# Latent-attention layer: probabilities times values as three float32r products, head squares on ScalarE, transposes moved

## The chip, the cores and the metric

The kernel runs on one core of one Trainium2 chip. The metric is the device time of one execution in microseconds. Before the change it is 2088.68 us, the median of three runs (2088.34 to 2089.35). All names of engines are those of the profile: PE is TensorE's matmuls and PEld its weight loads, DVE is VectorE, ACT is ScalarE, POOL is GpSimd, SP is SyncE, which issues the DMAs.

## What is computed

Two layers of a decoder trunk over 256 tokens of width 2048, all in float32. Each layer is attention and then a gated feed-forward network; layer 0 has block attention with 16 heads of 128, layer 1 multi-head latent attention. The change is in layer 1:

```python
def mla_attention(h, pos, wq_a, g_qa, wq_b, wkv_a, g_kva, wkv_b, g_qn, g_kn, g_qr, g_kr, wo):
    cq = rms_norm(h @ wq_a, g_qa)                        # 256 x 512
    q = (cq @ wq_b).reshape(B, S, H, NOPE + RD)          # 16 heads of 128 + 64
    q_nope = rms_norm(q[..., :NOPE], g_qn)
    q_rope = rope(rms_norm(q[..., NOPE:], g_qr), pos, RD)
    kv_a = h @ wkv_a
    ckv = rms_norm(kv_a[..., :MLA_KV_RANK], g_kva)
    k_rope = rope(rms_norm(kv_a[..., MLA_KV_RANK:], g_kr)[:, :, None, :], pos, RD)[:, :, 0]
    kv = (ckv @ wkv_b).reshape(B, S, H, NOPE + VD)
    k_nope = rms_norm(kv[..., :NOPE], g_kn)
    v = kv[..., NOPE:]
    s = (q_nope . k_nope + q_rope . k_rope) * scale      # causal, per head
    return softmax(s) @ v                                # then @ wo
```

## The kernel before

**Precision.** float32 matrices are split into two float32r parts, a high one (ScalarE rounds it, `whi`) and a low one (VectorE subtracts, `wlo`); a product is then three float32r matmuls: high by high, high by low, low by high. `three` and `feat_major` and `tok_major` do this. Where no parts are made, a float32 matmul is used; the trace shows such a matmul as two records.

**The stream of quanta.** Weights come in 1464 pieces of 128 x 512, in the order of their use. To each piece belongs one quantum of products. The order is written out by hand: for quantum q the program first issues work put `ahead`, then loads and splits weight pieces until four pieces lie ahead of q (`AHEAD_PIECES`; DMA by SP, high part by ACT at L104, low part by DVE at L105), then the products of q, and then side work: for each head the values and the turning of probabilities (`first_in`), and after them what `at(q, f)` has listed, in the order in which it was listed. Every engine works its own list in order, and waits by semaphores for what it reads and for buffers that others have yet to finish with.

**Layer 1** has 16 heads in four groups g of four. A group has twelve quanta, four each for k, q, v (group 0 has q, the rotary queries, k, v). A quantum of these is six matmuls of 512 columns (L239). The heads' scores, probabilities and values run as side work during the following groups and, for the last heads, during the output product (`plan_wo`, 12 matmuls of 256 columns a quantum, L265 to L267), which reads `oT`, the heads' outputs in parts.

`plan_heads` lays out what happens to one k or q of a group after its last product, at quantum q:

- q: `Heads.evac`, ACT copies 2 x 128 x 512 from PSUM to a tile `qk` (L376 for k, L378 for q). `qk` has two buffers in layer 1, used in turn by k, q, k, q and so on.
- q+1, q+2: `Heads.squares`, for each half of the tokens four DVE instructions with their accumulator reads (L383).
- q+3: `Heads.rstd`, DVE (L404) and POOL (L409).
- q+5, q+6: `Heads.scaled`, DVE (L414), one half of the tokens each.
- q+9, q+10: `Heads.turned`, two heads each, four PE transposes into one PSUM buffer (L462), and `turned_out`, ACT copies it with the gain into `room` (L473).

Only q of group 0 has other steps (`wide`). PSUM buffers for transposes (`tp`) are two, used in turn by `Heads.turned`, by the turning of probabilities (`Head.turn`, L536) and by the rotary queries.

`Head.plan` for a head whose scores are due at q0: scores (L499, L504) and mask with maximum (`biased`, DVE L510, L515) at q0; `exps` (ACT L519) at q0+1; `normal` (DVE L526, L528) at q0+2; `turn` and the copy of the transposed probabilities (ACT L542) at q0+6; `values` (L561, L562) and `parted` (ACT L568, DVE L569) at q0+9. In layer 1 the probabilities `pT` and the values are plain float32, the values in `room`; in layer 0 (`parts=True`) both are in parts and `values` is L477 to L479 and L559.

`room` is the space of the normalized input `h`, 32 slices of 128 x 256: queries, keys and values of layer 1.

Of the kernel before, what the change touches and what calls it, by code (L numbers as in the profile page):

```python
# [10 lines left out]
F32 = mybir.dt.float32  # L11
# [6 lines left out]
P = 128  # L18
# [30 lines left out]
BY_TOKEN, BY_FEATURE = (8, 8), (24, 56)  # L49

H_START = 8


class Stream:
# [61 lines left out]
def trunk(ctx: ExitStack, tc: tile.TileContext, a, out):  # L116
# [153 lines left out]
    class Norm:  # L270
# [6 lines left out]

        def high(self, j):
            if self.h is None:
                t = keep.tile([P, KD * 2 * S + 64], F32R, name="h")  # L280
                self.h = t[:, H_START : H_START + KD * 2 * S].rearrange("p (k s) -> p k s", k=KD)
# [75 lines left out]
    class Heads:  # L357


        def __init__(self, state, n_heads, dh, gain, rot, tabs, scale, gain_column=None):  # L360
            self.gain_column = gain_column
            self.state, self.n, self.dh, self.gain = state, n_heads, dh, gain
            self.rot, self.tabs, self.scale = rot, tabs, scale

        def evac(self):
            n, dh = self.n, self.dh
# [18 lines left out]
                    scalar=0.0, op0=ALU.mult, op1=ALU.add, accum_out=self.ss[:, t, i : i + 1],  # L385
                )

        def squared(self):

            self.sq = []  # L390
            for t in range(NT):
                sq = att_pool.tile([P, 16 * 32], F32, name="ro2", bufs=2)
                nc.scalar.activation(sq, self.x[:, t].rearrange("p n d -> p (n d)"), AF.Square)
                self.sq.append(sq.rearrange("p (n d) -> p n d", n=self.n))

        def sums(self, t):
            nc.vector.tensor_reduce(
# [77 lines left out]
    def three(o, w_hi, w_lo, m_hi, m_lo, start, stop):  # L475

        mm(o, w_hi, m_hi, start=start, stop=False)  # L477
        mm(o, w_hi, m_lo, start=False, stop=False)  # L478
        mm(o, w_lo, m_hi, start=False, stop=stop)  # L479


    class Head:
        def __init__(self, h, qT, kT, v, i, oT, scale, rope=None, parts=False):
            self.h, self.qT, self.kT, self.v, self.i = h, qT, kT, v, i
            self.oT, self.scale, self.rope, self.parts = oT, scale, rope, parts

        def scores(self):
            sc = ps_sc.tile([P, 512], F32, name="sc")
# [48 lines left out]
            self.tp = tp  # L537

        def turned(self):
            if not self.parts:  # L540
                self.pT = att_pool.tile([P, 3 * P], F32, name="pT", bufs=2)
                nc.scalar.copy(self.pT, self.tp[:, : 3 * P])  # L542
                return

            self.pT = att_pool.tile([P, 2, S], F32R, name="pT", bufs=2)
            self.pT1 = att_pool.tile([P, P], F32, name="pT1", bufs=2)
            hi, lo = self.pT[:, 0], self.pT[:, 1]
            nc.scalar.copy(hi, self.tp[:, :S])
            nc.scalar.copy(self.pT1, self.tp[:, S : 3 * P])
            nc.vector.tensor_tensor(lo, self.tp[:, :S], hi.bitcast(F32), op=ALU.subtract)  # L550

        def values(self):
            o = ps_sc.tile([P, 512], F32, name="sc")
            v = self.v()
            vs = slice(self.i * P, (self.i + 1) * P)
            if self.parts:
                v0, v1 = v
                three(o[:, :S], v0[:, 0, vs], v0[:, 1, vs], self.pT[:, 0], self.pT[:, 1], True, False)
                mm(o[:, P:S], v1[:, vs], self.pT1, start=False, stop=True)  # L559
            else:  # L560
                mm(o[:, :S], v[:, 0, vs], self.pT[:, :S], start=True, stop=False)  # L561
                mm(o[:, P:S], v[:, 1, vs], self.pT[:, S:], start=False, stop=True)  # L562
            self.o = o

        def parted(self):
# [66 lines left out]
    def evac_values(state, key, scale):  # L632
        for t in range(NT):
            dst, src = env[key][:, t, :], state["acc"][t][:, :512]
            if scale is None:
                nc.scalar.copy(dst, src)
            else:
                nc.scalar.activation(dst, src, AF.Copy, scale=scale()[:, t : t + 1])

    def plan_heads(q, hs, key, step, out=None, late=0, wide=False):  # L640

        at(q, hs.evac)
        if wide:
            for t in range(NT):
                for i in (0, 2):
                    at(q + 1 + 2 * t + i // 2, hs.squares, t, range(i, i + 2))
                at(q + 8 + t, hs.scaled, t)
            at(q + 5, hs.rstd)
            for i0 in (0, 2):
                pair = {}  # L650
# [7 lines left out]
        for t in range(NT):  # L658
# [359 lines left out]
    def rotary_queries(u, steps):  # L1018


        state = {}
        for kt in range(4):
            q = add(tok_major, state, lambda: env["cqT"], kt, 3)
        hs = Heads(state, 8, 64, None, 64, None, lambda: cq["scale"])
        steps = iter(q + n for n in steps)

        def rotate(t, stage):
            hs.tabs = (env["gtab"].rearrange("p a r -> p (a r)"), 0, NT * 64)
            hs.rotate(t, (stage,))

        at(q, hs.evac)
        at(q, hs.squared)
        for t in range(NT):
            at(next(steps), hs.sums, t)
        at(next(steps), hs.rstd)
        for t in range(NT):
            at(next(steps), hs.scaled, t)
        for t in range(NT):
            for stage in range(4):
                at(next(steps), rotate, t, stage)  # L1040
        for i0 in (0, 2):
            pair = {}
            n = next(steps)
            at(n, lambda p=pair, i0=i0: hs.turned(None, p, i0))
            parts = Rotary(pair, i0)
            at(n, parts.out, 0)
            at(n + 1, parts.out, 1)
# [29 lines left out]
    def mla_tiles(g):  # L1077
        i = 4 * (g % 2)
        env["qT", g] = env["room"][:, i : 4 + i]
        env["kT", g] = env["room"][:, 8 + i : 12 + i]  # L1080
        i = 4 * (g % 3)
        env["v", g] = env["room"][:, 16 + i : 20 + i].rearrange("p (t c) s -> p t (c s)", t=NT)

    for g in range(4):
        for kind in "kqv" if g else "qrkv":
            if kind == "r":
                rotary_queries(1, (6, 10, 12, 15, 16, 17, 18, 20, 21, 23, 24, 25, 26, 28, 40))
                continue
            state = {}
            for kt in range(4):  # L1090
                q = add(tok_major, state, lambda kind=kind: env["cqT" if kind == "q" else "ckvT"], kt, 3)
            if kind == ("k" if g else "q"):
                at(q, mla_tiles, g)
            if kind == "v":
                at(q, evac_values, state, ("v", g), None)
# [147 lines left out]
```

## Time and profile before

| what | value |
|---|---|
| median of the runs | 2088.68 us |
| the profiled execution, its own time | 2088.1 us |
| its span, first to last instruction | 2086.1 us |
| granted TensorE clock | 1.000 |
| layer 0, attention with its output product | 0 to 388 us |
| layer 0, feed-forward network | 388 to 1107 us |
| layer 1, low-rank products | 1107 to 1162 us |
| layer 1, q, k, v and heads | 1162 to 1259 us |
| layer 1, output product | 1259 to 1364 us |
| layer 1, feed-forward network | 1364 to 2086 us |

All profile lines are of that one execution, times in microseconds from the start of the span. Engines run side by side. A matmul's record lasts longer than the step to the next one, since matmuls are pipelined; what PE's work costs is read from start to start. Neighbouring records of DVE and of ACT overlap a little for the same reason. "idle before" is the rest of the engine ahead of an instruction, and the arrow names what ended it.

### The profile page before, as it was taken

What the parts mean: (1) busy time and instruction counts of PE and PEld (TensorE: products, weight loads), DVE (VectorE), ACT (ScalarE), POOL (GpSimd) and SP (SyncE); (2) the same over time, 40 slices, a digit from 0 to 9 for tenths busy, and PEclk for the clock granted to TensorE, in tenths of its full rate; (3) what the DMA queues carried; (4) which work ended last, traced back from release to release, by engine and by line L of the source; (5) the groups of instructions that cost most, each with busy time, mean ns of one, the idle gap of its engine ahead of it and who ended that gap; (6) DMA issues with size and microseconds to landing.
All of it is one profiled execution on the core that took longest, in us unless ns stands there. A gap on an engine that the chain in (4) does not pass through costs nothing.

```text
span 2086.1 us, 42075 instructions
## 1 busy us (share of the span) xinstructions
PE 2081.1 (100%) x16716; PEld 2012.4 (96%) x16716; DVE 1407.1 (67%) x3012; ACT 1133.3 (54%) x2199; POOL 46.1 (2%) x35
## 2 busy tenths in 40 slices
PE   9999999999999999999999999999999999999999
PEld 7888889999999999999999889999999999999999
DVE  6777776776666766655556886776676666755554
ACT  6555555555555555555455666655555555544443
POOL 0000000000000000000000110000000000000000
PEclk9999999999999999999999999999999999999999
DMA  7454445555555555555554533555555555555553
GB/s 274 162 182 176 168 162 202 183 194 190 202 186 200 191 194 199 191 197 189 197 202 154 200 122 122 183 201 185 200 193 191 200 187 200 190 202 208 195 207 132
DMA packets 59381, 391.81 MB, mean 188 GB/s; under 512 B 6960, under 2 KB 10032, under 8 KB 13232
## 3 DMA queue, kind: packets, MB, share of 16 engines
q1 hardware_dynamic: 59040, 388.87, 52.6%
q8 instruction: 130, 2.13, 0.4%
q14 instruction: 67, 0.55, 0.1%
q10 hardware_dynamic: 144, 0.26, 0.0%
HBM read 387.01 MB, written 2.10 MB: 187 GB/s over the span
## 4 chain that ended last, share of the span: by engine, by line
PE 99%; DMA 0%; SPq 0%; DVE 0%; ACT 0%; issue 0%
PE acc L265 26%; PE acc L267 26%; PE acc L266 26%; PE acc L239 17%; PE tp L462 1%; PE sc L499 1%; PE tp L536 1%; PE sc L561 0%; PE sc L504 0%; DMA xT<-in_xT 0%; PE sc L478 0%; PE sc L479 0%; PE sc L477 0%; PE sc L559 0%; PE sc L494 0%; PE sc L562 0%
## 5 line engine op out<-in xcount | busy, mean ns | idle before, releaser
L105 DVE TENSOR_TENSOR wlo<-raw,whi 128x512 fp32r<-128x512 f32 (+1 forms) x1464 | 999.5, 690 | 390.2 <-ACT whi L104 387.6
L104 ACT CAST whi<-raw 128x512 fp32r<-128x512 f32 (+1 forms) x1463 | 869.1, 619 | 456.3 <-PE acc L266 212.5
L265 PE MATMUL acc<-h,whi 128*128 128x256 f32 x2880 | 796.1, 276 | 0.0
L267 PE MATMUL acc<-h,wlo 128*128 128x256 f32 x2880 | 795.7, 276 | 0.0
L266 PE MATMUL acc<-h,whi 128*128 128x256 f32 x2880 | 795.6, 276 | 0.0
L266 PEld LDWEIGHTS acc<-h,whi 128*128 128x128 f32 x2880 | 540.8, 188 | 0.0
L267 PEld LDWEIGHTS acc<-h,wlo 128*128 128x128 f32 x2880 | 540.8, 188 | 0.0
L265 PEld LDWEIGHTS acc<-h,whi 128*128 128x128 f32 x2880 | 540.8, 188 | 0.0
L265 PE MATMUL acc<-a,whi 128*128 128x256 f32 x1408 | 389.0, 276 | 0.0
L266 PE MATMUL acc<-a,whi 128*128 128x256 f32 x1408 | 389.0, 276 | 0.0
L267 PE MATMUL acc<-a,wlo 128*128 128x256 f32 x1408 | 388.9, 276 | 0.0
L239 PE MATMUL acc<-whi,h 128*128 128x512 f32 (+1 forms) x896 | 272.6, 380 | 0.0
L267 PEld LDWEIGHTS acc<-a,wlo 128*128 128x128 f32 x1408 | 264.4, 188 | 0.0
L265 PEld LDWEIGHTS acc<-a,whi 128*128 128x128 f32 x1408 | 264.4, 188 | 0.0
L266 PEld LDWEIGHTS acc<-a,whi 128*128 128x128 f32 x1408 | 264.4, 188 | 0.0
L239 PEld LDWEIGHTS acc<-whi,h 128*128 128x128 f32 x896 | 164.8, 188 | 30.2 <-ACT whi L104 0.7
L239 PE MATMUL acc<-wlo,h 128*128 128x512 f32 (+1 forms) x448 | 168.8, 377 | 0.5 <-DVE wlo L105 0.5
L265 PE MATMUL acc<-oT,whi 128*128 128x256 f32 x512 | 142.7, 279 | 0.0
L267 PE MATMUL acc<-oT,wlo 128*128 128x256 f32 x512 | 141.7, 277 | 0.0
L266 PE MATMUL acc<-oT,whi 128*128 128x256 f32 x512 | 141.7, 277 | 0.0
L770 DVE TENSOR_TENSOR g<-acc,rstd_b 128x256 f32<-128x256 f32 x88 | 37.5, 426 | 125.4 <-PE acc L267 122.4
L777 ACT ACTIVATE c<-g,par 128x256 f32<-128x256 f32 x88 | 53.1, 603 | 108.3 <-DVE g L770 108.3
(163 smaller groups left out, 1599.6 us busy)
## 6 DMA issues: line engine op xcount, KB each, us to landing
raw<-in_ffn_gu SPq DMA_DIRECT2D x176, 1024.0 KB, 4.8
raw<-in_ffn_down SPq DMA_DIRECT2D x88, 1024.0 KB, 4.8
raw<-in_moba_wk SPq DMA_DIRECT2D x16, 1024.0 KB, 4.8
raw<-in_moba_wv SPq DMA_DIRECT2D x16, 1024.0 KB, 4.8
raw<-in_moba_wo SPq DMA_DIRECT2D x16, 1024.0 KB, 4.8
raw<-in_mla_wo SPq DMA_DIRECT2D x16, 1024.0 KB, 4.8
raw<-in_moba_wq SPq DMA_DIRECT2D x13, 1024.0 KB, 4.8
raw<-in_mla_wkv_a SPq DMA_DIRECT2D x8, 576.0 KB, 3.8
```

The lines of the kernel that those rows point to most:

```text
L104: self.nc.scalar.copy(hi[:, :n], w)
L105: self.nc.vector.tensor_tensor(lo[:, :n], w, hi[:, :n].bitcast(F32), op=ALU.subtract)
L239: mm(state["acc"][t][:, :n], src[:, kt, c : c + P], (t_lo if part == 1 else t_hi)[:, :n], start=kt == 0 and part == 0, stop=kt == k_last a ...
L265: mm(o, w_hi, src[:, kt, :S], start=first and k == 0, stop=False, skip_group_check=True)
L266: mm(o, w_hi, src[:, kt, S:], start=False, stop=False, skip_group_check=True)
L267: mm(o, w_lo, src[:, kt, :S], start=False, stop=kt == k_last, skip_group_check=True)
L462: nc.tensor.transpose(tp[:, (i * NT + t) * P : (i * NT + t + 1) * P], flat[:, t, c : c + P], ident)
L499: mm(o, qT[:, i, q0 : q0 + P], kT[:, i, :n], start=True, stop=self.rope is None)
L536: nc.tensor.transpose(tp[:, c * P : (c + 1) * P], self.s[:, c * P : (c + 1) * P], ident)
L770: nc.vector.tensor_tensor(self.g[:, 2:], self.gate["acc"][:, :S], self.norm.rstd_b, op=ALU.mult)
L777: nc.scalar.activation(self.c, self.g[:, 2:], AF.Identity, bias=par[:, cb : cb + 1], scale=self.cw(2))
```

## The change

In layer 1 alone:

- The values' first block of keys and the probabilities that meet it are made in parts; `values` becomes three float32r products of 256 columns and one float32 product of 128. The copy of the probabilities becomes two ACT copies and a DVE subtraction. The evacuation of the values gets a DVE subtraction.
- The squares of k's and q's heads are made by ACT (128 x 512, one for each half of the tokens, at q+1 and q+3) into one buffer `sq`, and summed by a DVE reduction at q+2 and q+4. `rstd` moves to q+4 (q+5 stays for group 0's q), `scaled` to q+6 and q+7.
- In groups 1 to 3 the transposes go from q+9 and q+10 to q+9 and q+12 for q, and to q+10 and q+14 for k.
- The last rotary queries' transposes move one quantum back (28 to 29, 40 to 41).
- `h` becomes two tiles, `h0` and `h1`, one for each half of the features. `room` takes the place of `h0` (queries and keys), `rparts` that of `h1` (values' parts and `pT`).

```diff
-        def squared(self):
-
-            self.sq = []
-            for t in range(NT):
+        def squared(self, t):
+
+            if self.dh == P:
+                sq = att_pool.tile([P, 16 * 32], F32, name="sq", bufs=1)
+            else:
                 sq = att_pool.tile([P, 16 * 32], F32, name="ro2", bufs=2)
-                nc.scalar.activation(sq, self.x[:, t].rearrange("p n d -> p (n d)"), AF.Square)
-                self.sq.append(sq.rearrange("p (n d) -> p n d", n=self.n))
+            nc.scalar.activation(sq, self.x[:, t].rearrange("p n d -> p (n d)"), AF.Square)
+            self.sq[t] = sq.rearrange("p (n d) -> p n d", n=self.n)
...
         def turned(self):
-            if not self.parts:
-                self.pT = att_pool.tile([P, 3 * P], F32, name="pT", bufs=2)
-                nc.scalar.copy(self.pT, self.tp[:, : 3 * P])
-                return
-
-            self.pT = att_pool.tile([P, 2, S], F32R, name="pT", bufs=2)
+
+            if self.latent:
+                i = 12 + 2 * (self.h % 2)
+                self.pT = env["rparts"][:, i : i + 2]
+            else:
+                self.pT = att_pool.tile([P, 2, S], F32R, name="pT", bufs=2)
             self.pT1 = att_pool.tile([P, P], F32, name="pT1", bufs=2)
...
-            if self.parts:
-                v0, v1 = v
-                three(o[:, :S], v0[:, 0, vs], v0[:, 1, vs], self.pT[:, 0], self.pT[:, 1], True, False)
-                mm(o[:, P:S], v1[:, vs], self.pT1, start=False, stop=True)
-            else:
-                mm(o[:, :S], v[:, 0, vs], self.pT[:, :S], start=True, stop=False)
-                mm(o[:, P:S], v[:, 1, vs], self.pT[:, S:], start=False, stop=True)
+            v0, v1 = v
+            three(o[:, :S], v0[:, 0, vs], v0[:, 1, vs], self.pT[:, 0], self.pT[:, 1], True, False)
+            mm(o[:, P:S], v1[:, vs], self.pT1, start=False, stop=True)
...
+        if scale is None:
+            nc.scalar.copy(hi, first_)
+            nc.vector.tensor_tensor(lo, first_, hi.bitcast(F32), op=ALU.subtract)
+            nc.scalar.copy(v1, second)
+            return
...
         at(q, hs.evac)
+        latent = out is None
+        if latent:
+            for t in range(NT):
+                at(q + 1 + 2 * t, hs.squared, t)
+                at(q + 2 + 2 * t, hs.sums, t)
         if wide:
+            at(q + 5, hs.rstd)
             for t in range(NT):
-                for i in (0, 2):
-                    at(q + 1 + 2 * t + i // 2, hs.squares, t, range(i, i + 2))
                 at(q + 8 + t, hs.scaled, t)
-            at(q + 5, hs.rstd)
...
+        if not latent:
+            for t in range(NT):
+                at(q + step * (1 + t), hs.squares, t)
+        at(q + step * 3 + latent, hs.rstd)
         for t in range(NT):
-            at(q + step * (1 + t), hs.squares, t)
-        at(q + step * 3, hs.rstd)
-        for t in range(NT):
-            at(q + step * (5 + t) + late * (1 + t), hs.scaled, t)
+            at(q + step * (5 + t) + late * (1 + t) + latent, hs.scaled, t)
             at(q + step * (5 + t) + late * (2 + t), hs.rotate, t)
         for i0 in (0, 2):
             pair = {}
             q1 = q + step * 9 + i0 // 2 + 2 * late
+            if latent and key[1]:
+                q1 = q + (9 + 3 * i0 // 2 if key[0] == "qT" else 10 + 2 * i0)
...
     def open_room():
-        t = keep.tile([P, KD * 2 * S + 64], F32, name="room", tag="h")
-        env["room"] = t[:, : 32 * S].rearrange("p (k s) -> p k s", k=32)
+
+        n = 16 * S
+        t = keep.tile([P, n + 64], F32, name="room", tag="h0")
+        env["room"] = t[:, :n].rearrange("p (k s) -> p k s", k=16)
+        t = keep.tile([P, n + 64], F32R, name="rparts", tag="h1")
+        env["rparts"] = t[:, H_START : H_START + n].rearrange("p (k s) -> p k s", k=16)
...
-        env["v", g] = env["room"][:, 16 + i : 20 + i].rearrange("p (t c) s -> p t (c s)", t=NT)
+        env["v", g] = (
+            env["rparts"][:, i : i + 4].rearrange("p (t c) s -> p t (c s)", t=2),
+            att_pool.tile([P, 512], F32, name="v1", bufs=3),
+        )
...
-                rotary_queries(1, (6, 10, 12, 15, 16, 17, 18, 20, 21, 23, 24, 25, 26, 28, 40))
+                rotary_queries(1, (6, 10, 12, 15, 16, 17, 18, 20, 21, 23, 24, 25, 26, 29, 41))
```

More of the change, by code (lines that the diff above doesn't have):

```diff
@@ L51, with __init__, __getitem__ @@
 H_START = 8
+class Halves:
+    def __init__(self, tiles):
+        self.tiles = tiles
+    def __getitem__(self, at):
+        p, k, s = at
+        return self.tiles[k // 8][p, k % 8, s]
 class Stream:
@@ L279, in high @@
             if self.h is None:
-                t = keep.tile([P, KD * 2 * S + 64], F32R, name="h")
-                self.h = t[:, H_START : H_START + KD * 2 * S].rearrange("p (k s) -> p k s", k=KD)
+                n = KD // 2 * 2 * S
+                tiles = [keep.tile([P, n + 64], F32R, name=f"h{i}") for i in range(2)]
+                self.h = Halves([
+                    t[:, H_START : H_START + n].rearrange("p (k s) -> p k s", k=KD // 2) for t in tiles
+                ])
             g = par[:, self.gain_col + j : self.gain_col + j + 1]
@@ L363, in __init__ @@
             self.rot, self.tabs, self.scale = rot, tabs, scale
+            self.sq = {}
         def evac(self):
@@ L485, in __init__ @@
             self.oT, self.scale, self.rope, self.parts = oT, scale, rope, parts
+            self.latent = rope is not None
         def scores(self):
@@ L654, in plan_heads @@
             return
+        if not latent:
+            for t in range(NT):
+                at(q + step * (1 + t), hs.squares, t)
+        at(q + step * 3 + latent, hs.rstd)
         for t in range(NT):
-            at(q + step * (1 + t), hs.squares, t)
-        at(q + step * 3, hs.rstd)
-        for t in range(NT):
-            at(q + step * (5 + t) + late * (1 + t), hs.scaled, t)
+            at(q + step * (5 + t) + late * (1 + t) + latent, hs.scaled, t)
             at(q + step * (5 + t) + late * (2 + t), hs.rotate, t)
@@ L1031, in rotary_queries @@
         at(q, hs.evac)
-        at(q, hs.squared)
+        for t in range(NT):
+            at(q, hs.squared, t)
         for t in range(NT):
@@ L1094, in trunk @@
             if kind == "v":
-                at(q, evac_values, state, ("v", g), None)
+                at(q, evac_parts, state, ("v", g), None)
             else:
```

6 lines of the change are left out of this document (removed).

## The prediction

> **What bounds the kernel now.** I read the page first, then the wait chain, then layer 1 by windows, by groups and in order of time.
>
> ```profile
> span 2086.1 us, 42075 instructions
> PE 2081.1 (100%) x16716; PEld 2012.4 (96%) x16716; DVE 1407.1 (67%) x3012; ACT 1133.3 (54%) x2199; POOL 46.1 (2%) x35
> PE 99%; DMA 0%; SPq 0%; DVE 0%; ACT 0%; issue 0%
> ```
>
> The rows are the span, the engines' busy time and the chain that ended last: 99% of the chain is TensorE (PE) following itself. A microsecond is won only where PE has less to stream, and lost wherever PE is made to wait. The changed stage in windows (columns: window, us, then busy us of PE, weight loads, DVE, ACT, POOL; clock; DMA share; GB/s):
>
> ```profile
> 1200.00:1215.00 15.00, 15.00 (x85) 12.96 (x83) 13.28 (x49) 9.65 (x25) 2.63 (x2) 1.00 0.39 142
> 1230.00:1245.00 15.00, 15.00 (x85) 12.97 (x84) 14.29 (x60) 11.19 (x30) 1.94 (x1) 1.00 0.33 132
> ```
>
> PE never rests at full clock (1.00), but VectorE (DVE) is busy 13.28 and 14.29 us of 15 and ScalarE (ACT) 9.65 and 11.19. PE is kept fed only because both run some quanta ahead of it, so here the order of their work decides, not its sum. DMA, at 0.33 to 0.39, is off the path.
>
> **Values as three products.** Rows in order of time (start us, us, engine, line, names, count); first a head of layer 0, which already uses three products, then one of layer 1.
>
> ```profile
> 97.69 0.28 PE L477 MATMUL sc<-pT,v 128*128 128x256 f32 x1
> 97.81 0.28 PE L478 MATMUL sc<-pT,v 128*128 128x256 f32 x1
> 97.92 0.28 PE L479 MATMUL sc<-pT,v 128*128 128x256 f32 x1
> 98.05 0.39 PE L559 MATMUL sc<-pT,v 128*128 128x128 f32 x2
> 98.27 0.49 PE L536 MATMUL tp<-ident,s 128*128 128x128 f32 x3
> 1213.27 0.59 PE L561 MATMUL sc<-pT,room 128*128 128x256 f32 x2
> 1213.70 0.38 PE L562 MATMUL sc<-pT,room 128*128 128x128 f32 x2
> 1213.92 0.49 PE L536 MATMUL tp<-ident,s 128*128 128x128 f32 x3
> ```
>
> Matmuls overlap, so I cost by starts. Values plus the step to the next transpose take 98.27 - 97.69 = 0.58 us in layer 0 and 1213.92 - 1213.27 = 0.65 us in layer 1. The gain is 0.07 us for each of 16 heads: **-1.1 us**. Bounds: 0 (the new operands, side by side in one tile, might read slower) and -1.3 (0.08 a head, the rows' rounding). [...]
>
> Each transpose group keeps its size and number. Moving it costs PE nothing in itself: a group of four takes the same 0.36 us wherever it stands (rows 1216.74 and 1217.10 below).
>
> **The squares.** From the groups of layer 1 (xcount | busy us, mean ns | idle before):
>
> ```profile
> L383 DVE CUSTOM_DVE_ANT_0 junk<-qk 128x128 f32<-128x128 f32 x64 | 14.9, 286 | 0.0
> L397 DVE TENSOR_REDUCE ss<-ro 128x8 f32<-128x512 f32 x2 | 1.4, 678 | 0.0
> L393 ACT ACTIVATE ro<-qr 128x512 f32<-128x512 f32 x2 | 1.2, 638 | 0.0
> L569 DVE TENSOR_TENSOR oT<-sc,oT 128x256 fp32r<-128x256 f32 x13 | 5.5, 422 | 3.3 <-ACT oT L568 3.2
> ```
>
> Sixty-four head squares leave DVE. Neighbours overlap by about 0.08 us, so each costs about 0.21 us with its accumulator read: 13.4 us. Sixteen sums come instead at 0.68 - 0.08 = 0.60: 9.6 us. New on DVE are also the low parts of the probabilities (0.42 - 0.08 = 0.34 for each of 16 heads, shape of L569) and of the values (about 0.6 for each of 4 groups): 7.8 us. Net DVE **+4 us** in about 140 us; ACT gets sixteen squares at some 0.55 us, **+9 us**, and the copy of the probabilities in two pieces. None of it is on PE's path as long as the lead lasts, so it is priced at nothing by itself; what it costs when the lead is gone comes now.
>
> **A new wait of ACT on PE.** Quanta of layer 1 come in groups of twelve: four k, four q, four v. The tile "qk" has two buffers, taken in turn by k and q, so k of the next group gets the buffer of k of this one. In groups 1 to 3, k's second transposes move from q+10 to q+14, but the next group's evacuation (L376) still stands at q+12. It overwrites what those transposes have yet to read, and must wait for them, about two quanta. Today the evacuations wait for their own product alone, little:
>
> ```profile
> L376 ACT COPY qk<-acc 128x512 f32<-128x512 f32 x8 | 4.5, 594 | 1.3 <-PE acc L239 1.1
> ```
>
> It happens twice (k of group 1 against group 2, of 2 against 3; q's second transposes, at q+12, stand in the list ahead of the evacuation of that quantum). Behind the blocked copy ACT holds, in order: the second half of the evacuation, a cast of weights, two exponentials, then the copy that empties the transpose buffer of q's first group. That buffer is one of two; k's second transposes take the other, so the next head's transposes (L536) need this one. Rows for the chain, ACT then PE:
>
> ```profile
> 1215.18 1.08 ACT L376 COPY qk<-acc 128x512 f32<-128x512 f32 x2
> 1216.13 0.65 ACT L104 CAST whi<-raw 128x512 fp32r<-128x512 f32 x1
> 1218.17 0.40 ACT L519 ACTIVATE s<-s,sst 128x128 f32<-128x128 f32 x1 [1.39 <-DVE sst L515]
> 1219.06 0.67 ACT L473 ACTIVATE room<-tp,par 128x512 f32<-128x512 f32 x1
> 1219.63 0.61 ACT L104 CAST whi<-raw 128x512 fp32r<-128x512 f32 x1
> 1220.14 0.68 ACT L473 ACTIVATE room<-tp,par 128x512 f32<-128x512 f32 x1
> 1216.74 0.60 PE L462 MATMUL tp<-ident,qk 128*128 128x128 f32 x4
> 1217.10 0.47 PE L239 MATMUL acc<-whi,cqT 128*128 128x512 f32 x1
> 1218.56 0.60 PE L462 MATMUL tp<-ident,qk 128*128 128x128 f32 x4
> ```
>
> ACT needs 1216.13 - 1215.18 = 0.95 for the evacuation, 1220.14 - 1219.63 = 0.51 for the cast, 1219.06 - 1218.17 = 0.89 for the exponentials and 0.67 for the copy: 3.02 us. It starts when the transposes end, 1216.74 + 0.60, which is 0.24 after the next product starts at 1217.10; so it is done 3.3 us after that start. PE, meanwhile, runs one quantum (1218.56 - 1217.10 = 1.46) and the values (0.58), and stands at the head's transposes after 2.04. It waits about 1.3 us, twice: **+2.6 us**. Bounds: +0.8, were the exponentials out of that chain (0.89 less each); +5.4, if they still wait for DVE as the row at 1218.17 does (1.39 more each).
>
> **Scaling a quantum later.** The scaling of k and q (L414) moves back one quantum, q's first transposes stay at q+9. DVE today around one such group:
>
> ```profile
> 1201.23 0.69 DVE L105 TENSOR_TENSOR wlo<-raw,whi 128x512 fp32r<-128x512 f32 x1 [1.44 <-ACT whi L104]
> 1211.85 0.17 DVE L515 TENSOR_SCALAR sst<-sst 128x2 f32<-128x2 f32 x1
> 1211.92 0.68 DVE L414 TENSOR_TENSOR qk<-qk,hr 128x512 f32<-128x512 f32 x1
> 1213.13 0.69 DVE L414 TENSOR_TENSOR qk<-qk,hr 128x512 f32<-128x512 f32 x1
> 1214.16 0.69 DVE L105 TENSOR_TENSOR wlo<-raw,whi 128x512 fp32r<-128x512 f32 x1 [0.34 <-ACT whi L104]
> 1215.56 0.55 DVE L528 TENSOR_SCALAR s<-s,sst 128x128 f32<-128x128 f32 x2
> 1216.03 0.69 DVE L105 TENSOR_TENSOR wlo<-raw,whi 128x512 fp32r<-128x512 f32 x1
> ```
>
> The second scaling ends at 1213.82, 2.9 us ahead of the transposes at 1216.74. In its new place it follows the normalization at 1215.56, so it would start where the cast stands now, 1216.03, and end at 1216.72, just as the second transpose of the four, some 0.1 after 1216.74, wants it: 0.1 us spare. Since DVE's last long rest (1201.23, 1.44 us) it would also have done two sums (+1.2), one low part of values (+0.6) and one of probabilities (+0.3), against eight head squares gone (-1.7): 0.4 us later. ACT's extra square ahead of the cast that ends such a rest adds up to 0.5, say 0.3. PE comes 0.4 sooner, since k's second group (0.36) now stands behind that place and a head's values are 0.07 shorter. Together 1.1 - 0.1 = 1.0 us for group 1, and the same again for group 2; group 3's fall into the output product, whose lead I price below. **+2.0 us**, bounds 0.3 (DVE's count alone, once) and 3 (half as much again).
>
> **What else runs dry.** With DVE about 0.8 us later (0.4 + 0.3 above, rounded up), leads below that turn into waits. The first output quantum:
>
> ```profile
> 1258.34 0.69 DVE L105 TENSOR_TENSOR wlo<-raw,whi 128x512 fp32r<-128x512 f32 x1
> 1259.29 0.28 PE L267 MATMUL acc<-oT,wlo 128*128 128x256 f32 x1
> 1264.14 0.42 DVE L569 TENSOR_TENSOR oT<-sc,oT 128x256 fp32r<-128x256 f32 x1
> 1265.94 0.28 PE L266 MATMUL acc<-oT,whi 128*128 128x256 f32 x1
> ```
>
> A low part done at 1259.03 is used at 1259.29: lead 0.26, so some 0.5 is lost there. Head 7's low part, done at 1264.56, is read at 1265.94: lead 1.4. DVE's 0.8, a rotary part moved one quantum back (about 0.6) and a low part of probabilities (0.3) use it up and leave some 0.3. With a like sum for the leads between, I take **+1.2 us**, bounds 0 and 3.
>
> **Sum.** -1.1 + 2.6 + 2.0 + 1.2 = +4.7 us. The profiled execution took 2088.1 us (span 2086.1 and 2.0 around it), 0.6 under the median 2088.68 and inside the runs' noise; 2088.1 + 4.7 = 2092.8 on its own footing, 2093.4 against the median. Split tiles of h, the rotary steps and the larger room change no PE product and are priced in the terms above.
>
> **Rivals.**
> - *Leads hold (faster or no change).* DVE loses more in squares than it gains before PE needs it, ACT's block ends before PE reaches the transposes; only -1.1 stays: 2087.6. For it: ACT has some 4 us free in 15. Against it: the block is by order, not by load, and ACT works its list in order. [...]
> - *The block spreads (slower still).* While ACT stands still for some two quanta it casts no weights; the four quanta of lead shrink to about two, and DVE's low part waits on each late cast. If each of the two stops also costs a whole product quantum (1.46), 2.9 us come on top: 2096.3. Decided where PE's product after the head's block waits for whi or wlo. For it: windows with DVE at 14.29 of 15 leave no room to catch up. Against: two casts still lie ahead of the block.
> - *The products don't shrink.* The second product needs the low part of the probabilities, DVE's new 0.42 us behind two ACT copies; if it is late by that in every head, 16 x 0.4 = 6.4 us come back: 2093.4 + 6.4 = 2099.8. Against: transposes and values stand three quanta, over 4 us, apart.
> - *Layout.* Half of h and all behind it move by a few hundred bytes; a change of 1 ns on each of 16716 matmuls would be 17 us either way, 2076 or 2110. Against: the rows give no sign that spacing hangs on place; 2093.4 stays the middle.
>
> **How the numbers follow.** Forecast 0.64, leads hold 0.13, block spreads 0.17, products late 0.03, layout 0.03. The forecast's own range is 2091.5 to 2095.5. The 8-in-10 range reaches into the neighbours on both sides: 2089.5 to 2097.5. A difference of 0.2%, 4.2 us, is about what a measurement of this kernel can tell from none, so "slower" begins at 2092.9. Of the forecast 0.47 lies above it and 0.17 below. Slower: 0.47 + 0.17 + 0.03 and half of layout, 0.69; same: 0.13 + 0.17, 0.30; faster: the other half, 0.01.
>
> **What would show it.** In the profile after: the evacuation copy (L376's successor) idle for about 3.5 us twice, released by PE's transposes of qk; PE waiting over 1 us before a head's transposes, released by ACT's copy into room, twice; PE waiting about 1 us at q's first transposes, released by DVE's scaling of qk; values at 0.58 a head. Wrong if PE has no wait of over 0.5 us between 1160 and 1310 us, or if the largest sits elsewhere, before whi or the second product of the values.

## The result and the profile after

| | before | after |
|---|---|---|
| median of 7 runs, us | 2088.68 | 2095.07 |
| lowest to highest, us | 2088.34 to 2090.05 | 2094.62 to 2096.51 |
| profiled run, its span, us | 2088.1, 2086.1 | 2095.44, 2093.4 |

The ratio of the runs is 1.003, with a 95% interval of 1.002 to 1.004: the changed kernel is slower by 6.4 us, 0.3%. The prediction said 2093.4 with 2089.5 to 2097.5.

The span, the engines' busy time and the chain that ended last, after:

```profile
span 2093.4 us, 42070 instructions
PE 2081.8 (99%) x16732; PEld 2011.7 (96%) x16732; DVE 1411.4 (67%) x2920; ACT 1142.3 (55%) x2231; POOL 43.8 (2%) x35
PE 96%; DVE 2%; ACT 1%; DMA 1%; issue 0%; SPq 0%; ACTq 0%; DVEq 0%
```

The first row is the span, the second each engine's busy time, the third the chain. PE's busy time is about what it was (2081.1), the span is 7.3 us longer. PE was 99% of the chain and is now 96%: the loss is time in which PE waits. To place it I take two marks on PE, layer 1's first scores and the transposes of that layer's second `rstd`, ahead of its feed-forward network. Rows in order of time (start us first), before and then after:

```profile
1196.36 0.38 PE L499 MATMUL sc<-room 128*128 128x128 f32 x2
...
1369.65 0.43 PE L340 MATMUL tp<-ident,rstd 128*128 128x128 f32 x2
```

```profile
1197.34 0.38 PE L516 MATMUL sc<-room 128*128 128x128 f32 x2
...
1377.00 0.43 PE L354 MATMUL tp<-ident,rstd 128*128 128x128 f32 x2
```

From mark to mark the kernel took 1369.65 - 1196.36 = 173.3 us and takes 179.7: **6.4 us more, all of the difference of the medians**. The other 1.0 us of the profiled spans arises ahead of the first scores, and nothing ties it to the change: in the profiled runs below these start anywhere from 1196.49 to 1198.57, with no relation to the edit. So the table of experiments gives this stretch beside the medians.

The waits of PE between 1150 and 1330 us, after (engine, line waited for: us in total, times, longest):

```profile
PE tp L553 <- ACT room L489: 2.3, 2, 1.2
PE tp L478 <- DVE qk L430: 1.9, 2, 1.3
PE acc L277 <- DVE oT L582: 1.0, 1, 1.0
PE acc L250 <- DVE wlo L116: 0.5, 1, 0.5
```

Before, this view has no line: all four are new. They are the copy into `room` (ACT), the scaling (DVE), head 7's low part (`oT`, DVE) and a low part of weights (`wlo`, DVE). The first of the waits for the copy into `room`, ACT above, PE below:

```profile
1217.10 0.28 ACT L566 COPY pT<-tp 128x128 f32<-128x128 f32 x1
1221.21 1.08 ACT L391 COPY qk<-acc 128x512 f32<-128x512 f32 x2 [3.83 <-PE tp L478]
1222.17 0.63 ACT L115 CAST whi<-raw 128x512 fp32r<-128x512 f32 x1
1222.69 0.41 ACT L536 ACTIVATE s<-s,sst 128x128 f32<-128x128 f32 x1
1223.58 0.68 ACT L489 ACTIVATE room<-tp,par 128x512 f32<-128x512 f32 x1
```

```profile
1220.57 0.60 PE L478 MATMUL tp<-ident,qk 128*128 128x128 f32 x4
1222.76 0.38 PE L575 MATMUL sc<-pT,v 128*128 128x128 f32 x2
1224.31 0.55 PE L553 MATMUL tp<-ident,s 128*128 128x128 f32 x3 [1.17 <-ACT room L489]
```

This is the predicted chain. ACT is free at 1217.4 and its next work, the evacuation of the next group's keys, overwrites the buffer that PE reads until 1220.57 + 0.60. ACT rests 3.83 us, then works off the cast, the exponentials and the copy that frees the transposes' buffer, and the head's transposes start at 1224.31 in place of 1222.98 (1222.76 and two steps of 0.11). That is 1.33 us late; the view counts 1.17, since it takes a record's end for the end of work. It happens once more, 30 us later: 3.22 us of rest ahead of ACT's copy, 1.17 ahead of PE's transposes at 1254.51. The other long waits of PE:

```profile
1217.23 0.27 PE L478 MATMUL tp<-ident,qk 128*128 128x128 f32 x1
1218.79 0.55 PE L478 MATMUL tp<-ident,qk 128*128 128x128 f32 x3 [1.29 <-DVE qk L430]
1248.17 0.27 PE L478 MATMUL tp<-ident,qk 128*128 128x128 f32 x1
1249.01 0.44 PE L478 MATMUL tp<-ident,qk 128*128 128x128 f32 x2 [0.56 <-DVE qk L430]
1242.33 0.62 PE L250 MATMUL acc<-whi,ckvT 128*128 128x512 f32 x2
1243.50 0.50 PE L250 MATMUL acc<-wlo,ckvT 128*128 128x512 f32 x1 [0.55 <-DVE wlo L116]
1272.13 0.28 PE L276 MATMUL acc<-oT,whi 128*128 128x256 f32 x1
1273.42 0.38 PE L277 MATMUL acc<-oT,whi 128*128 128x256 f32 x1 [1.02 <-DVE oT L582]
```

Read from start to start, less the usual step (0.11 for transposes and products of 256 columns, 0.23 for those of 512): the scaling costs 1.45 and 0.73, `wlo` 0.71, head 7's low part 1.18. These prices are larger than the view's; the step-by-step table below goes by them.

### The profile page after: what moved, and what is told of

Its sections match the earlier page's. It is cut to its first block, busy times and chain, and to the rows that moved or that the text cites. A ratio compares the mean times of both kernels' runs of the same rounds, so it can differ in the third digit from the quotient of the medians.

```text
span 2093.4 us, 42070 instructions
## 1 busy us (share of the span) xinstructions
PE 2081.8 (99%) x16732; PEld 2011.7 (96%) x16732; DVE 1411.4 (67%) x2920; ACT 1142.3 (55%) x2231; POOL 43.8 (2%) x35
## 4 chain that ended last, share of the span: by engine, by line
PE 96%; DVE 2%; ACT 1%; DMA 1%; issue 0%; SPq 0%; ACTq 0%; DVEq 0%
PE acc L278 26%; PE acc L277 26%; PE acc L276 26%; PE acc L250 15%; PE tp L478 1%; DMA raw<-in_moba_wq 1%; DVE wlo L116 0%; PE tp L553 0%; DMA xT<-in_xT 0%; PE sc L516 0%; PE sc L575 0%; ACT whi L115 0%; PE sc L494 0%; PE sc L495 0%; PE sc L493 0%
```

## The experiments

Each row is one kernel; "V", "S" and "M" are the values as three products, the squares on ACT and the moved transposes. The stretch is that between the two marks; "more" stands against the kernel before of the same comparison and the 173.3 us.

| kernel | median us | more | stretch more | ratio, 95% |
|---|---|---|---|---|
| changed: V, S, M | 2095.07 | 6.4 | 6.4 | 1.002 to 1.004 |
| S alone | 2089.09 | 0.2 | 0.1 | 0.9991 to 1.0009 |
| M alone | 2092.92 | 4.0 | 4.1 | 1.0011 to 1.0028 |
| V alone | 2090.33 | 1.5 | 1.9 | 0.9998 to 1.0016 |
| V alone, no low parts | 2087.20 | -1.7 | -1.2 | 0.9982 to 0.9999 |
| V and S | 2090.16 | 1.3 | 1.7 | 0.9999 to 1.0016 |
| V and M | 2094.08 | 5.3 | 5.0 | 1.0016 to 1.0037 |
| V, S, M, no low parts | 2090.97 | 2.1 | 2.6 | 1.0002 to 1.0020 |
| V, S, M, keys' second at q+12 | 2091.70 | 2.9 | 2.9 | 1.0005 to 1.0023 |
| V, S, M, keys' second at q+13 | 2093.93 | 5.1 | 5.0 | 1.0017 to 1.0037 |
| V, S, M, queries at q+10, q+13 | 2096.26 | 7.4 | 7.6 | 1.0022 to 1.0047 |
| V, S, keys and queries at q+9, q+11 | 2089.03 | 0.1 | 0.3 | 0.9992 to 1.0010 |
| the same, rotary on GpSimd | 2093.03 | 4.2 | 3.6 | 1.0010 to 1.0028 |

An interval reaches about 2 us to either side, so a difference of 1.5 by the runs alone is not told from none; the stretch of the one profiled execution agrees with the median's within 0.6 in every row.

**The wait for the qk buffer.** The keys' second transposes two quanta sooner, nothing else:

```diff
-                q1 = q + (9 + 3 * i0 // 2 if key[0] == "qT" else 10 + 2 * i0)
+                q1 = q + (9 + 3 * i0 // 2 if key[0] == "qT" else 10 + i0)
```

> The changed kernel with one edit: the second transposes of a group's keys two quanta sooner (q + 12 in place of q + 14), so that the next group's copy into that qk buffer finds them issued in its own quantum. The prediction's term: ScalarE's wait for the qk buffer falls from 7.0 us to under 1, the two waits of PE for the copy into room go (2.7 us), and the scaling's waits stay at about 2: 2095.1 - 2.7 = 2092.4. Rival 1, ScalarE's wait also makes the casts late that VectorE and PE then wait for: the scaling's waits, wlo and oT's head 7 shrink with it, 4 to 5 us in all, 2090 to 2091. Rival 2, the loss is in more separate groups of transposes, not in waits: 2094.5 to 2095.5.

Measured: 2091.70, 3.4 us less than the changed kernel. ACT and the waits of PE there (between 1150 and 1330 us):

```profile
1216.96 0.71 ACT L489 ACTIVATE room<-tp,par 128x512 f32<-128x512 f32 x1
1217.55 1.09 ACT L391 COPY qk<-acc 128x512 f32<-128x512 f32 x2
```

```profile
PE acc L277 <- DVE oT L582: 1.0, 1, 1.0
PE acc L250 <- DVE wlo L116: 0.5, 1, 0.5
PE tp L478 <- DVE qk L430: 0.4, 1, 0.4
PE tp L478 <- DVE rparts L567: 0.3, 1, 0.3
PE tp L478 <- ACT room L489: 0.2, 1, 0.2
```

The copy no longer rests and the room copy's two waits of the head's transposes are gone: the predicted 2.7. The scaling's waits shrink from 1.9 to 0.4, against which two small new ones (0.3 and 0.2) stand at the transposes. The keys' second group, 0.36 us of PE's work and some 0.08 of changing over (the product behind it steps 0.31 and not 0.23), now stands one quantum ahead of the queries' first and fills that much of each wait for the scaling. The gain of 3.4 is less than the rival's 4 to 5, and `wlo` and head 7 stay as they were: the blocked copy was not their cause.

At q + 13:

```diff
+                q1 = q + (9 + 3 * i0 // 2 if key[0] == "qT" else 10 + 3 * i0 // 2)
```

> The changed kernel with the keys' second transposes at q + 13, between the q + 12 of the kernel that lost 2.9 us and the q + 14 of the change. ScalarE's wait for the qk buffer should be about one quantum with a head's block shorter than the 3.8 and 3.2 us, and the time between 2091.7 and 2095.1: 2093. Rival, a threshold: any quantum after the copy's own costs all of the 3.4 us, 2094.5 to 2095.5; or none of it, 2091.7.

Measured: 2093.93, in between, but not for the reason given. ACT no longer rests at that copy; PE waits 4.4 us in three places, for a low part:

```profile
PE tp L478 <- DVE rparts L567: 4.4, 3, 2.3
```

Here the keys' second group and the next queries' first fall into one quantum, six products after a head's transposes and scores, and there are two transpose buffers for the three. The queries' group needs the head's, which is free only when DVE has made the low part of the probabilities, listed behind a scaling and two low parts. So the place counts for two rings of two buffers, `qk` and `tp`.

**One part alone.** The kernel before with the moves alone (the new line of `plan_heads` and the rotary steps 29 and 41):

```diff
+            if out is None and key[1]:
+                q1 = q + (9 + 3 * i0 // 2 if key[0] == "qT" else 10 + 2 * i0)
...
-                rotary_queries(1, (6, 10, 12, 15, 16, 17, 18, 20, 21, 23, 24, 25, 26, 28, 40))
+                rotary_queries(1, (6, 10, 12, 15, 16, 17, 18, 20, 21, 23, 24, 25, 26, 29, 41))
```

> The kernel before with only the transposes moved (keys q + 10 and q + 14, queries q + 9 and q + 12, the last two of the rotary queries 29 and 41). The prediction's term: ScalarE's wait for the qk buffer holds the copy into room and so the head's transposes, 1.3 us twice: 2088.8 + 2.6 = 2091.4, and ScalarE's idle time ahead of the copies into qk of 3.5 us or so twice. Rival: alone it is covered by the lead of the kernel before, 2088.5 to 2089.5, and the loss comes only together with the new subtractions.

Measured: 2092.92, 4.0 more. The stage's waits, of PE and then of ACT:

```profile
PE tp L536 <- ACT room L473: 2.2, 2, 1.1
PE acc L239 <- DVE wlo L105: 0.5, 2, 0.2
...
ACT qk L376 <- PE tp L462: 7.7, 2, 4.2
```

The mechanism is there without the other two parts, ACT resting even longer. The 1.4 beyond the predicted 2.6 is at low parts of weights. From start to start three products stand 0.41, 0.38 and 0.28 us for them (at 1234.60, 1238.56 and 1267.42), and each product behind steps 0.11 or 0.12 later than usual; the view shows only 0.5 of this. Whether the two stops of ACT made these low parts late is not shown.

The squares alone (the new `squared`, `sums` and the shift of `rstd` and `scaled` by one quantum, in the kernel before):

```diff
+                at(q + 1 + 2 * t, hs.squared, t)
+                at(q + 2 + 2 * t, hs.sums, t)
...
+            at(q + step * (5 + t) + late * (1 + t) + latent, hs.scaled, t)
```

> The kernel before with only the squares of the latent heads on ScalarE, summed by VectorE in one instruction, and with them the scaling one quantum later; values and transposes as before. The prediction laid the waits for the scaling (2.0) to this edit: 2088.8 + 2 = 2090.8. Rival: without the other edits there is lead enough, the edit costs nothing by itself, and PE waits nowhere: 2088.3 to 2089.2.

Measured: 2089.09, 0.2 more, and the view of PE's waits has no line between 1150 and 1330 us. The edit to which the prediction laid 2.0 us costs nothing by itself.

The values alone (`values`, `turned`, `evac_parts` and the two tiles of `h` as changed, all else as before):

```diff
-                mm(o[:, :S], v[:, 0, vs], self.pT[:, :S], start=True, stop=False)
+            three(o[:, :S], v0[:, 0, vs], v0[:, 1, vs], self.pT[:, 0], self.pT[:, 1], True, False)
...
+            nc.vector.tensor_tensor(lo, first_, hi.bitcast(F32), op=ALU.subtract)
```

> The kernel before with only the three-product values (and the two halves of h that go with them): squares by VectorE and all transposes in their old quanta. The prediction's term: PE saves 0.07 us in each of 16 heads and nothing new waits: 2088.7 - 1.2 = 2087.5. Rival: with the squares still on VectorE, its new subtractions (a low part for each head and each group's values) make wlo or the copies into room late, 1 to 3 us: 2088.5 to 2090.5.

Measured: 2090.33, 1.5 more and not 1.2 less: the rival. The runs alone would not tell 1.5 from none; the stretch is 1.9 longer, and PE has waits in the stage:

```profile
PE tp L478 <- ACT room L489: 1.3, 3, 0.6
PE acc L250 <- DVE wlo L116: 0.8, 1, 0.8
```

The copy into `room` is ACT's, but DVE stands behind its delay: ahead of the longest of these waits ACT rests 3.23 us for the maxima that its exponentials need (at 1236.61), and DVE makes these behind two low parts, one of them new. From there ACT works without a rest until that copy.

The same kernel without its 20 new subtractions. All three products then multiply high parts, so the first block of values comes out threefold; the kernel only prices the subtractions:

```diff
-            nc.vector.tensor_tensor(lo, self.tp[:, :S], hi.bitcast(F32), op=ALU.subtract)
+            if not self.latent:
+                nc.vector.tensor_tensor(lo, self.tp[:, :S], hi.bitcast(F32), op=ALU.subtract)
...
-            three(o[:, :S], v0[:, 0, vs], v0[:, 1, vs], self.pT[:, 0], self.pT[:, 1], True, False)
+            l = 0 if self.latent else 1
+            three(o[:, :S], v0[:, 0, vs], v0[:, l, vs], self.pT[:, 0], self.pT[:, l], True, False)
...
-            nc.vector.tensor_tensor(lo, first_, hi.bitcast(F32), op=ALU.subtract)
```

> The values-alone kernel without the subtractions that make the low parts of the probabilities (16) and of layer 1's first block of values (4): the three products run on the high parts alone, so PE does the same work and the output lacks the low parts' terms. If VectorE's 20 new subtractions make the loss of the values-alone kernel: 2088.8 - 1.2 = 2087.6, with no wait of PE left in layer 1. Rival, the loss there is ScalarE's second copy for a head, or the h in two tiles: 2089.5 to 2090.5 as with them.

Measured: 2087.20, no wait of PE in the stage. The busy time of DVE, the third number behind the window's length (PE, weight loads, DVE), over the first 59 or 60 us from the first scores, without the subtractions and with them:

```profile
1196.00:1255.00 59.00, 59.00 (x339) 51.11 (x337) 49.95 (x196) 43.37 (x110) 10.48 (x6) 1.00 0.34 121
```

```profile
1198.00:1258.00 60.00, 58.40 (x329) 49.68 (x328) 52.44 (x200) 41.88 (x109) 10.10 (x6) 1.00 0.33 117
```

The twenty subtractions raise DVE from 85% of the stage to 87%, and cost 3.1 us of PE's time (2090.33 - 2087.20, and the same by the stretch), more than the 1.7 that the products save. Without them DVE also no longer reads the transposes' buffer, which is free sooner for that, but no wait of PE in the kernel with them names that reading (L567): here it is DVE's list that is late. The same edit on the whole changed kernel:

> The whole changed kernel without the 16 subtractions for the probabilities' low parts and the 4 for the values' (the three products run on high parts alone; the output lacks the low parts' terms). If the parts add, the moves' 4.0 and PE's saving of 1.7 are left: 2088.9 + 4.0 - 1.7 = 2091.2, with PE's two waits for the copy into room there and those at oT's head 7, wlo and the scaling gone. Rival, the waits at the scaling and the room copy are as long without the subtractions: 2092.5 to 2094.

Measured: 2090.97. The two waits for the room copy stay at 2.3, that for the scaling falls to 0.4 (from start to start 0.54 and 0.28, where it was 1.45 and 0.73), those for `wlo` and head 7 are gone. So 4.1 us of the changed kernel hang on the twenty subtractions. What is left, 2.1, is about the moves' 4.0 less the products' 1.7.

**Two parts together.** The changed kernel with the squares back on DVE:

```diff
-                at(q + 1 + 2 * t, hs.squared, t)
-                at(q + 2 + 2 * t, hs.sums, t)
...
+            at(q + step * (1 + t), hs.squares, t)
-        at(q + step * 3 + latent, hs.rstd)
+        at(q + step * 3, hs.rstd)
```

> The changed kernel with the squares of the latent heads back on VectorE and the scaling back in its old quantum; values and moved transposes as changed. The prediction laid 2.0 us of scaling waits to the squares' edit: 2095.1 - 2 = 2093.1, with no wait at the queries' first transposes. Rival, the waits there come from the new subtractions and ScalarE's late casts, whoever squares: the time stays at 2094.5 to 2095.5.

Measured: 2094.08, 1.0 less than with the squares on ACT, half of what was expected. The waits of PE between 1160 and 1330:

```profile
PE tp L553 <- ACT room L489: 2.3, 2, 1.2
PE acc L250 <- DVE wlo L116: 1.2, 2, 0.6
PE acc L278 <- DVE wlo L116: 0.6, 1, 0.6
```

The scaling's line is gone and `wlo` has grown in its place: DVE has the squares of single heads to do again, and another of its products is now the one for which PE stands. By the medians the squares on ACT thus cost 1.0 here and nothing alone; by the stretch it is 1.4. The runs by themselves would not tell that from none.

The changed kernel with the old transposes:

```diff
-            if latent and key[1]:
-                q1 = q + (9 + 3 * i0 // 2 if key[0] == "qT" else 10 + 2 * i0)
...
+                rotary_queries(1, (6, 10, 12, 15, 16, 17, 18, 20, 21, 23, 24, 25, 26, 28, 40))
```

> The changed kernel with the transposes of keys and queries, and the last two of the rotary queries, put back to their old quanta (q + 9 and q + 10; 28 and 40); values and squares stay as changed. The prediction's terms: the wait for the qk buffer goes (-2.7), the scaling's two waits stay (about 2), of the rest (2.5 more that runs dry) about half goes: 2091. Rival 1, moving the transposes apart is what the other two parts need: without it the waits move but do not shrink, 2094 to 2096. Rival 2, the move alone makes the loss and values save 1.2: about 2087.5.

Measured: 2090.16, below the expected 2091. ACT does not rest at the copy into `qk`, and the scaling still has 1.0 us of waits, the room copy 0.9. From here the moves cost 4.9 (2095.07 - 2090.16), from the values alone 3.8, from the kernel before 4.0.

**Trying to mend it.** The queries' transposes of the changed kernel a quantum later:

```diff
+                q1 = q + (10 + 3 * i0 // 2 if key[0] == "qT" else 10 + 2 * i0)
```

> The changed kernel with one edit: the transposes of a group's queries one quantum later (q + 10 and q + 13 in place of q + 9 and q + 12). The prediction's term: PE's two waits for the scaling of qk (1.45 and 0.72 us by start to start in the changed kernel) go and nothing else does: 2095.1 - 2.1 = 2093.0. Rival: what PE waits for there is VectorE and ScalarE behind the head's steps, not the extra quantum of the squares; a quantum later another wait of 1 to 2 us stands in its place, at the head's transposes or scores: 2094.5 to 2096.5.

Measured: 2096.26, the rival. The waits for the scaling are gone, the room copy's have doubled, and a new one stands at the transposes (1.7 us of the profiled stretch are another matter, the clock, shown in the last part):

```profile
PE tp L553 <- ACT room L489: 4.8, 4, 1.8
PE tp L478 <- DVE rparts L567: 0.9, 1, 0.9
```

Keys' and queries' transposes both in q+9 and q+11, the rotary steps as before:

```diff
-                q1 = q + (9 + 3 * i0 // 2 if key[0] == "qT" else 10 + 2 * i0)
+                q1 = q + ((9, 11)[i0 // 2] if key[0] == "qT" else (9, 11)[i0 // 2])
```

> The changed kernel with other quanta for the transposes: keys and queries both at q + 9 and q + 11, the last two of the rotary queries at 28 and 40 as before. The keys are then read before the next copy into their buffer is due, and the two groups of transposes are still not in neighbouring quanta. By the experiments so far the wait for the qk buffer (3.4) goes, and with the second transposes one quantum from the first the room copy's wait at 1239 of the kernel with old quanta (1.0) goes too: 2089 at most, 2088 if nothing else runs dry. Rival, some other wait of 1 us or more stands in their place: 2090 to 2091.

Measured: 2089.03 against 2088.91, ratio 1.0001. 6 us of the change's loss come back, with 0.9 us of waits left in the stage, but it doesn't beat the kernel before: its stretch is 0.3 longer than before where PE's products alone would make it 1.2 shorter. To take work from DVE, the eight rotary instructions went to GpSimd:

```diff
+            eng = nc.gpsimd if self.gain is None else nc.vector
...
-                nc.vector.tensor_tensor(t1, x[:, :, :rot], over(ct), op=ALU.mult)
+                eng.tensor_tensor(t1, x[:, :, :rot], over(ct), op=ALU.mult)
```

> The kernel of 2089.0 (keys and queries at q + 9 and q + 11) with the rotary queries' 8 multiplications and additions of layer 1 on GpSimd, idle there but for the powers, in place of VectorE. If VectorE's load is what still makes the scaling and oT late (0.5 us three times), PE waits less and the time comes to 2087.5 to 2088.3, below the kernel before's 2088.9. Rival, GpSimd is too slow for its steps or slows VectorE down, and the rotary queries' transposes wait: 2090 or more.

Measured: 2093.03, the rival, by way of VectorE: PE stands 2.7 us at the queries' first transposes, and the clock falls to 0.50 behind that wait, as in the kernel with the queries later (last part). No kernel tried that does the whole computation beats the one before.

## Why the prediction was nearly right

The sign, the size and the main mechanism held; the time was 1.7 us above the forecast and in its own range. Step by step:

| step | predicted us | in the changed kernel | by experiment |
|---|---|---|---|
| values as three products, PE | -1.1 | 1214.39 - 1213.81 = 0.58 a head | -1.7 (stretch -1.2) |
| wait of ACT for `qk` | +2.6 | 1.33 and 1.33 | M alone: +4.0 in all |
| scaling a quantum later | +2.0 | 1.45 and 0.73 | S alone: +0.2 |
| what else runs dry | +1.2 | `wlo` 0.71, head 7 1.18, rest about 0.9 | not apart: with the scaling's part, 20 subtractions cost 4.1 |
| sum | +4.7 | +6.4 | |

- *The products* were right: the stretch without low parts is 1.2 us shorter. The rows say the same, 0.58 us a head. The median of that kernel gives 1.7 (2088.91 - 2087.20), but within 2 us it can't part 1.7 from 1.2; the stretch gives 1.2, and the rows, 0.07 for each of 16 heads, 1.1.
- *The wait for the `qk` buffer* was right in place, chain, idle time (3.83 and 3.22 for "about 3.5, twice") and price: ACT needs 1224.26 - 1221.21 = 3.05 us from the copy's start to the end of the copy into `room`, where 3.02 was predicted. Shown by taking it away (keys at q + 12) and by the moves alone.
- *The scaling* had the right size (2.18 for 2.0, by luck over two groups, 1.45 and 0.73 where 1.0 each was forecast) and only a part of the cause. The prediction laid it to the squares' extra quantum; without the other edits that quantum is covered. It takes all three: with the squares and the scaling back in their old places no wait for it is left, though others grow (2094.08); with the twenty subtractions gone 0.4 is left by the view; with the keys' transposes sooner 0.4 as well. The step that failed is "Together 1.1 - 0.1 = 1.0 us for group 1, and the same again for group 2", booked under the scaling's move: what it added up, sums, subtractions and late casts, belongs to all three edits.
- *What else runs dry* was mis-sized: 1.2 was taken with bounds of 0 and 3; some 2.8 came (0.71 + 1.18 = 1.89, and the remainder, 6.4 + 1.2 - 2.66 - 2.18 - 1.89 = 0.9). Head 7 was given 0.3 and took 1.18: ahead of it DVE now has a sum (L413, 0.68) and a low part of values (L640, 0.68), and the working for that place carried DVE's delay over from the scaling's place and counted neither.
- *The load on the helpers* came out as priced: DVE 1407.1 to 1411.4 for "+4", ACT 1133.3 to 1142.3 for "+9". *Squares priced at nothing by themselves*: right. *Values' new work on DVE priced at nothing while the lead lasts*: wrong, since the lead does not last even without the other edits; it costs 3.1 alone, in a stage where DVE is busy 85% of the time.
- *The rivals.* "Leads hold" fell. "The block spreads" (2096.3) was to show in a wait for `whi` or `wlo` behind the head's block; there is one of 0.71 in one group, not a quantum in each. "The products don't shrink" and "layout" fell: values take their 0.58, and the squares alone and the values without low parts show nothing of 1 ns a matmul.

Of the last 0.9 us most stands beside the long waits: the first products behind `wlo` and head 7 step 0.11 late, the rotary queries' transposes at 1229.19 start 0.20 late, and the product at 1239.48 and the one behind it 0.06 and 0.11. What isn't settled: what these last three wait for, and whether a third `qk` buffer would make q + 14 free; that wasn't tried.

## What to carry to other kernels

Where an in-order engine refills one of two buffers by a written schedule, moving the last reader of a buffer past the quantum of its refill blocks everything listed behind the refill, whatever its average load (here, with the moves alone, ACT rested 7.7 us in two places and the kernel lost 4.0): look for reader and refill as a pair before moving either. On a helping engine that is 85% busy, an instruction isn't free just because it is off PE's path: here twenty subtractions cost 3.1 us, more than the 1.7 that the products they made possible saved. And a wait is seen at the first consumer that needs the late engine, so its line names the place, not the edit that made it late; only undoing the edits one by one parted the two.

## What the hardware showed

*The granted clock fell to 0.50 behind two of PE's long rests, and not behind a third.* In the kernel with the queries a quantum later PE stood 1.8 us at one place between 1251 and 1254. Windows around it (window, us, then busy us of PE, weight loads, DVE, ACT, POOL; then the granted clock):

```profile
1251.00:1254.00 3.00, 1.22 (x10) 0.95 (x8) 1.61 (x4) 3.00 (x9) 0.00 (x0) 1.00 0.32 63
1254.00:1255.00 1.00, 0.97 (x7) 0.77 (x5) 1.00 (x4) 1.00 (x4) 0.00 (x0) 0.73 1.04 442
1255.00:1256.00 1.00, 1.00 (x4) 0.82 (x4) 1.00 (x3) 1.00 (x4) 0.00 (x0) 0.50 0.97 410
1256.00:1257.20 1.20, 1.20 (x6) 1.01 (x5) 0.88 (x5) 0.44 (x1) 0.00 (x0) 0.50 0.07 21
1257.20:1258.00 0.80, 0.80 (x4) 0.67 (x3) 0.77 (x5) 0.54 (x3) 0.00 (x0) 0.57 0.00 0
1258.00:1262.00 4.00, 4.00 (x23) 3.38 (x22) 0.79 (x3) 1.55 (x4) 1.64 (x1) 1.00 0.00 0
```

Against a clock of 1.00 the four windows from 1254 to 1258 lack 0.27 + 0.50 + 0.60 + 0.34 = 1.7 us, by estimate the cost beside the wait itself. The kernel with the rotary steps on GpSimd has the same after its wait of 2.7 us: the windows of 1 us from 1222 on show clocks of 0.81, 0.50, 0.50 and 0.50, another 1.7 us. Yet after the longest wait of the kernel with the keys at q + 13 (2.3 us by the view above) it stayed at 1.00:

```profile
1218.00:1221.00 3.00, 0.74 (x7) 0.51 (x6) 2.96 (x9) 1.74 (x4) 0.00 (x0) 1.00 0.01 3
1221.00:1222.00 1.00, 1.00 (x7) 0.89 (x7) 0.96 (x7) 0.11 (x1) 0.00 (x0) 1.00 0.00 0
```

So the length of a rest alone does not decide: the half clock followed rests of 1.8 and 2.7 us, and not the one of 2.3. The kernel alone does not either: over a whole run the granted clock of the kernel with the keys at q + 13 is 0.999 in five of its nine runs and 1.000 in the other four, the profiled one among them. What decides is not shown.

*VectorE's steps took longer beside GpSimd's.* In the last kernel, VectorE beside GpSimd's rotary steps:

```profile
1214.80 1.30 POOL L470 TENSOR_TENSOR qr<-ro,ro 128x512 f32<-128x512 f32 x1
1216.06 1.80 POOL L464 TENSOR_TENSOR ro<-qr,gtab 128x512 f32<-128x512 f32 x1
```

```profile
1215.17 0.96 DVE L533 TENSOR_SCALAR sst<-sst 128x2 f32<-128x2 f32 x1
1216.64 1.77 DVE L430 TENSOR_TENSOR qk<-qk,hr 128x512 f32<-128x512 f32 x1
1220.41 1.75 DVE L430 TENSOR_TENSOR qk<-qk,hr 128x512 f32<-128x512 f32 x1
```

The scaling takes 1.77 where it took 0.68 (1211.92 in the kernel before), a tiny scalar step 0.96 where it took 0.17 (1211.85), and PE waited 2.7 us at the queries' transposes, released by the second of these scalings. The first scaling starts at 1216.64, beside GpSimd's step of 1216.06 to 1217.86, and ends at 1218.41, 0.55 after that step. Not every step of VectorE took longer: a low part of weights at 1216.04, beside the same step, took its usual 0.68. What held the others is not shown.
